# Branch C's query projections one by one, lower bounds in layer 0's MLP, and three changes of tiles in a hybrid encoder

## The chip, the cores and the metric

The kernel runs on one core of a Trainium2 chip as one program. Its engines are TensorE (PE, with weight loads shown as PEld), VectorE (DVE), ScalarE (ACT), GpSimd (POOL) and SyncE (SP); each takes its instructions in the order in which they stand in its queue. The metric is the device time of one execution in microseconds (us), and the profile is of one execution of its own.

## What is computed

A bidirectional encoder of two layers on 512 positions of 1024 channels. The reference, cut to what bears on the change:

```
for l in range(DEPTH):
    xn = rms_norm(x, ln1[l])
    z = xn @ w_in[l]                 # all branches' inputs at once
    a_q, a_i, a_ff, a_fb, a_g, b_u, b_v, c_q, c_k, c_v, gz = jnp.split(z, offsets, axis=-1)
    o_a = hgrn2_bidirectional(a_q, a_i, a_ff, a_fb, lower[l])   # 4 heads, both directions
    ...
    qh = partial_rope(c_q.reshape(bsz, s_len, C_QHEADS, C_HDIM), pos)   # 8 heads of 64
    y_c = window_attention(qh, kh, vh, sink[l])                 # |i - j| <= 128
    merged = gates[..., 0] * (y_a @ w_br[l, 0]) + gates[..., 1] * (y_b @ w_br[l, 1]) + gates[..., 2] * (y_c @ w_br[l, 2])
    x = x + merged @ w_out[l]
    x = x + jnp.square(jax.nn.relu(rms_norm(x, ln2[l]) @ w_up[l])) @ w_down[l]
p = softmax(lb_logits, axis=0); cum = cumsum(p, axis=0)
lower = cum - cum[0:1]               # 0 in layer 0: only layer 1 needs the lower bounds
```

## The kernel before

Each weight comes from memory as a chunk of 128x1024 (`wr` or `wq`, loads on SP's queue), is rounded by ACT (`wh`, L210) and its remainder is taken by DVE (`wl`, L211). A projection of 128 output channels is then 24 matmuls of 512 columns, three for each of eight parts of the inner dimension (L215 to L217), into one bank of PSUM; `evac` multiplies it by the norm's factor on DVE (L739) and frees the bank. The banks "m", from which most projections come, are two, so a projection waits for the evacuation of the last but one.

The order on each engine is not the order of the code. A scheduler places the instructions by priorities and a timeline of its own: what is written earlier has the higher priority, `hp()` raises it, and `with later(30000)` lowers it, so that the work in it (`fill`, the projections and gates of branch B) stands between other work. Where a tile's slots are taken (`SLOTS`, a number for each tag), a new tile of that tag waits for a release.

A layer runs in this way. First come the products common to all (`seven`), then head 0 of branch A (`a_head`) with branch B's mixing. `project(1)` follows, then the projections `ck`, `cv` and all four `cq` of branch C, each for two heads. From there `head(1)`, `head(2)`, `head(3)` go through `overlap`: seven levels of one head of A, each with attention matmuls `at` and sums over `ex` on DVE (L614), together with the tail of the head before (`kT`, `stp`, `av`, `oT`) and with one step of `c_run`, which is one pair of score blocks of C (`sc`, softmax on DVE and ACT, then `pT` and `po`). `c_q(j)` rotates a query: `rot` shuffles it on DVE, multiplies by `sin_t` on DVE and by `cos_t` on POOL (L950), adds on DVE, and splits it into halves on ACT and DVE (L988, L989). Between heads stand `fill(0, 1)`, `fill(2, 3)`, and at the end `fill(4, 5, 6, 7)`; each number is a projection `gz`, a product `yB` and a store to `mgd` on POOL's queue. Last come `gate_a` (`ag`), branch C's gated product (`yC`; gates are loaded to `th` from `thd` on POOL's queue, the first half is kept in `kept`, the second is stored to `mcd`), branch A's product (`yA`), the transposes `mT`, the output projection `wo` and the MLP (`up`, and `dA`, `dB`, `dC`).

`lower_bounds` makes three 128x8 constants from the logits in `vec_t`: small DVE rows, two Exp and two Ln on ACT, each change of function with a table load. It is written behind head 0 of layer 0, and its first tile is of the tag "a", which the pool of the branches owns.

Of the kernel before, what the change touches and what calls it, by code (L numbers as in the profile page):

```python
# [7 lines left out]
F32R = mybir.dt.float32r  # L8
# [52 lines left out]
def trunk(tc, xT, xt, ws, vec, fnb, bsb, snk, wst, rope, cmask, amask, ident, out):  # L61
# [4 lines left out]
    def pool(**kw):  # L66
# [13 lines left out]
    SLOTS = {"x": 16, "l": 8, "l2": 4, "tv": 8, "rb": 1, "jk": 1,  # L80
             "xs": 16, "zt": 6,
             "yh": 8,
             "q": 2, "a": 6, "ao": 1, "g": 2, "ch": 10,
             "yi": 16, "th": 8, "mg": 4,
             "h": 22}

# [6 lines left out]
    def nm(s):  # L93
        ctr[0] += 1
        return f"{s}_{ctr[0]}"

    def T(tag, name, dt=F32):
        where = part[HOME[tag]] if tag in HOME else sb
        return where.tile([P, S], dt, tag=tag, bufs=SLOTS[tag], name=nm(name))
# [22 lines left out]
    def SM(tag, w):  # L122
        return pad.tile([P, w], F32, tag="sm_" + tag, bufs=4 if tag == "lb" else NSM, name=nm(tag))
# [61 lines left out]
    def wload(*key):  # L185
        if key in ready:
            return ready.pop(key)
        with hp():
            raw = sb.tile([P, CW], F32, tag="wr", bufs=WR, name=nm("wr"))
            nc.sync.dma_start(raw, ws[CHUNK[key]])  # L190
            return wsplit(raw)
# [35 lines left out]
    def proj(xs, name, *key, bank="m"):  # L227

        return proj_w(xs, name, wload(*key), bank=bank)

    def proj_w(xs, name, w, koff=0, bank="m"):
        hi, lo = w
        pt = PT(bank, name)
        for k, x in enumerate(xs):
            c = slice((koff + k) * P, (koff + k + 1) * P)
            mm3(pt, hi[:, c], lo[:, c], x[0], x[1], k == 0, k == len(xs) - 1)
        return pt
# [251 lines left out]
    def lower_bounds():  # L489

        a, b = vec_t[:, 42:50], vec_t[:, 50:58]
        V = nc.vector
        m = T("a", "lbm")[:, 0:8]
        V.tensor_tensor(m, a, b, ALU.max)
        ea, eb = SM("lb", 8), SM("lb", 8)
        V.tensor_tensor(ea, a, m, ALU.subtract)
        V.tensor_tensor(eb, b, m, ALU.subtract)
        nc.scalar.activation(ea, ea, AF.Exp)
        nc.scalar.activation(eb, eb, AF.Exp)
        s = SM("lb", 8)  # L500
        V.tensor_tensor(s, ea, eb, ALU.add)
        V.reciprocal(s, s)
        V.tensor_tensor(ea, ea, s, ALU.mult)
        V.tensor_tensor(eb, eb, s, ALU.mult)
        lb = SM("lb", 8)
        V.tensor_tensor(lb, ea, eb, ALU.add)
        V.tensor_tensor(lb, lb, ea, ALU.subtract)
        om = SM("lb", 8)
        V.tensor_scalar(om, lb, -1.0, 1.0, ALU.mult, ALU.add)
        res = []  # L510
        for i, src in enumerate((om, lb)):
            g, z = SM("lb", 8), SM("lb", 8)
            V.tensor_scalar(z, src, 0.0, -1.0e30, ALU.is_le, ALU.mult)
            V.tensor_scalar(g, src, 1e-38, None, ALU.max)
            nc.scalar.activation(g, g, AF.Ln)
            r = cst.tile([P, 8], F32, name=f"lbr{i}")
            V.tensor_tensor(r, g, z, ALU.add)
            res.append(r)
        dl = cst.tile([P, 8], F32, name="lbd")
        V.tensor_tensor(dl, res[0], res[1], ALU.subtract)  # L520
        return res[0], res[1], dl
# [155 lines left out]
    def steps(run, n):  # L677
        for _ in range(n):
            with hp():
                next(run)  # L680

    def overlap(run, tail, side):

        for i in range(len(LEVELS)):
            steps(run, 1)
            if i < 4:
                steps(tail, 1)
            if i:
                next(side, None)


    begin("wq")
# [11 lines left out]
    raw, hi, lo = sb.tile([P, CW], F32, tag="wr", bufs=WR, name=nm("wr")), *whl()  # L704
# [21 lines left out]
    lbs = None  # L726
# [6 lines left out]
    for l in range(DEPTH):  # L733
        xs = n1.xs

        def evac(pt, tag, name):
            t = T(tag, name)
            with hp():
                nc.vector.tensor_tensor(t, pt, n1.rb, ALU.mult)  # L739
            return t  # L740
# [111 lines left out]
        for u in range(3):  # L852
            nxt = uload(l, "un", u + 1) if u < 2 else None
# [29 lines left out]
        oa = []  # L883
        run = a_head(l, 0, *head_0, vt, oa)
        steps(run, len(LEVELS))
        if l == 0:
            lbs = lower_bounds()

        for i in range(4):
            gelu2(bu[i])  # L890
        for t in range(4):
# [54 lines left out]
        def rot(z):  # L946
            sh = T("g", "sh")
            nc.vector.stream_shuffle(sh, z, list(range(8, 16)) + list(range(8)) + list(range(16, 32)))
            nc.vector.tensor_tensor(sh, sh, sin_t, ALU.mult)
            nc.gpsimd.tensor_tensor(z, z, cos_t, ALU.mult)  # L950
            nc.vector.tensor_tensor(z, z, sh, ALU.add)
            return z
# [2 lines left out]
        def project(h):  # L955
            return a_ffb(h), evac(proj(xs, "q", l, "q", h), "q", "q")

        def head(h, gq):
            nonlocal run
            nxt = a_head(l, h, *gq, vt, oa)  # L960
            overlap(nxt, run, banded)
            run = nxt

        head_1 = project(1)
        lo64, hi64 = slice(0, 64), slice(64, 128)
        ck = evac(proj(xs, "ck", l, "ck"), "ch", "ck")
        cvT = evac(proj(xs, "cv", l, "cv"), "ch", "cv")
        cq = [evac(proj(xs, "cq", l, "cq", j), "ch", "cq") for j in range(4)]
        ck = rot(ck)
        k2 = [T("tv", "k2", F32R), T("tv", "k2", F32R)]  # L970

# [10 lines left out]
        nc.scalar.copy(cv, pt)  # L982

        def c_q(j):
            z = rot(cq[j])
            qs = [T("ch", "q2", F32R), T("ch", "q2", F32R)]
            for h, (r, o) in enumerate(((lo64, hi64), (hi64, lo64))):
                nc.scalar.copy(qs[h][r], z[r])  # L988
                nc.vector.tensor_tensor(qs[h][o], z[r], qs[h][r].bitcast(F32), ALU.subtract)  # L989
            return qs  # L990
# [61 lines left out]
        def fill(*ds):  # L1052
            with later(30000):
                for d in ds:
                    merge_b(d)
# [13 lines left out]
            c_out(*prev)  # L1069

        banded = c_run()
        head(1, head_1)
        fill(0, 1)
        head(2, project(2))
        fill(2, 3)
        head(3, project(3))
# [4 lines left out]
        with later(30000):  # L1081
            for h in range(4):
                gate_a()

            ys = y_split(yc, "yh")
            kept = []
            for fl in range(2):
                th = gates("ch", 0, fl)
                pts = proj_tok(ys, "yC", (l, "y", 2, fl), 0)
                for t in range(4):  # L1090
                    if fl == 0:
                        kept.append(T("tv", "mC"))
                    m = th[t] if fl else kept[t]
                    with hp():
                        nc.vector.scalar_tensor_tensor(m, th[t], 1.0, pts[t], ALU.add, ALU.mult)
                    if fl:
                        nc.gpsimd.dma_start(mcd[:, t], m)
        ys = []
        for h in range(4):
            nc.vector.scalar_tensor_tensor(oa[h], oa[h], 0.5, sg[h], ALU.mult, ALU.mult)  # L1100
            hi, lo = T("tv", "yh", F32R), T("l", "yl", F32R)
            split(oa[h], hi, lo)
            ys.append((hi, lo))
        end("br")
# [53 lines left out]
        i = proj_part(n2.xs, *first[0], range(4))  # L1158
# [51 lines left out]

        for qd in range(4):
            hs, nh = [], [0]

            def new():
                nh[0] += 1
                return T("jk" if nh[0] == 1 else "rb" if nh[0] > 27 else "l2" if nh[0] > 23 else "h", "sh", F32R)

            for f in range(8):
                if qd == 0 and f < 3:
                    pt = first[f][0]  # L1220
                    proj_part(n2.xs, *first[f], range(4, KT))
                else:
                    pt = proj(n2.xs, f'up{qd}', l, "up", qd, f, bank="c" if qd == 0 and f == 3 else "m")
                if f == 0:
                    raw = uload(l, "dn", qd)
                u = Z()
                with hp():
                    nc.scalar.activation(u, pt, AF.Relu)
                    nc.scalar.activation(u, u, AF.Square)
                    if f % 2 == 0:  # L1230
                        hs.append(left_first(new, u))
                    else:
                        left_second(new, hs[-1], u)
                if f == (6 if qd == 0 else 4):
                    with tc.issue_after(hs[1]["i"].ins) if qd == 0 else contextlib.nullcontext():
                        early_sums(raw)
            if qd == 3:
                if last:
                    for fl in range(2):
                        fn_t.append(Z())  # L1240
                        nc.sync.dma_start(fn_t[fl], bass.AP(tensor=fnb.tensor, offset=fnb.offset + fl * S, ap=[[0, P], [1, S]]))
                else:
                    nxt = uload(l + 1, "un", 0)
            down(qd, raw, hs, acc, xr, r2, nr2, done, last)
# [129 lines left out]
```

## Time and profile before

| What | us or share |
|---|---|
| median of 3 runs (1717.69 to 1720.3) | 1719.31 |
| the profiled execution | 1723.92 |
| its span, first to last instruction | 1722.1 |
| mean granted TensorE clock | 0.993 |
| PE busy | 1686.2 (98%) |
| DVE busy | 1297.3 (75%) |
| ACT busy | 1017.0 (59%) |
| POOL busy | 137.3 (8%) |

Times in the views count from the first instruction. The branches of layer 0 run from about 186 to 430, those of layer 1 from about 1040 to 1300; the rest is the common products and the MLP. In a view by stretches PE's pauses are the stretch less its busy time, and PEclk is the share of full clock that was granted. A row of the timeline has its start, its duration, and in brackets the idle time of the engine just before it and what ended it.

### The profile page before, as it was taken

The page shows a single profiled execution, that of the slowest core. Times are in us where ns is not written, and L with a number is a line of the kernel's source. Part 1 is how long each engine was busy: PE and PEld are TensorE (multiplying, and loading weights), DVE is VectorE, ACT ScalarE, POOL GpSimd, SP SyncE. Part 2 cuts the span into 40 slices and gives each one's busy share as a digit, 9 for nine tenths or more (in the row PEclk, how much of TensorE's full clock was granted, in tenths as well). Part 3 has the DMA queues.
Part 4 walks back from the last instruction along what each step waited for, and adds up shares of the span by engine and source line. Part 5 has one row for each costly group of instructions (what it writes and reads, how often), then busy time and mean ns, then how long its engine had stood idle before and what let it go on. Part 6 is the DMA issues. An engine that isn't in the chain of part 4 may idle for free.

```text
span 1722.1 us, 21872 instructions
## 1 busy us (share of the span) xinstructions
PE 1686.2 (98%) x8024; PEld 1407.6 (82%) x8024; DVE 1297.3 (75%) x2009; ACT 1017.0 (59%) x1717; POOL 137.3 (8%) x199
## 2 busy tenths in 40 slices
PE   8999989999999999999999999999999999999998
PEld 7888878888778888888888788778887888888886
DVE  7996997775566758686889869968845667686867
ACT  7665677765235554545665757588753355545454
POOL 0011111100210000000010111110003100000001
PEclk9999999999999999999999999999999999999999
DMA  9342212222545323232323422122325452223321
GB/s 332 98 144 92 86 58 102 68 92 74 186 181 183 110 99 98 98 98 98 135 98 122 148 103 74 56 92 80 101 74 183 164 195 98 98 98 98 112 72 49
DMA packets 57003, 195.84 MB, mean 114 GB/s; under 512 B 7648, under 2 KB 8032, under 8 KB 56896
## 3 DMA queue, kind: packets, MB, share of 16 engines
q1 hardware_dynamic: 44640, 154.72, 26.7%
q0 software_dynamic: 11968, 39.20, 6.4%
q8 instruction: 63, 1.03, 0.2%
q10 hardware_dynamic: 288, 0.52, 0.1%
q14 instruction: 44, 0.36, 0.1%
HBM read 175.54 MB, written 18.87 MB: 113 GB/s over the span
## 4 chain that ended last, share of the span: by engine, by line
PE 79%; issue 7%; DVE 6%; ACT 4%; DMA 2%; POOL 1%; POOLq 0%; SPq 0%; ACTq 0%; DVEq 0%
PE up L216 7%; PE up L215 7%; PE up L217 7%; PE dA L430 3%; PE dA L431 3%; PE dA L432 3%; PE at L572 2%; PE wo L265 2%; PE wo L266 2%; PE wo L267 2%; PE dC L431 2%; PE dC L430 2%; PE dC L432 2%; PE po L1039 2%; PE f L215 1%
## 5 line engine op out<-in xcount | busy, mean ns | idle before, releaser
L210 ACT CAST wh<-wq 128x1024 fp32r<-128x1024 f32 x201 | 211.5, 1053 | 206.7 <-PE dA L431 48.3
L211 DVE TENSOR_TENSOR wl<-wq,wh 128x1024 fp32r<-128x1024 f32 x201 | 244.9, 1221 | 114.8 <-ACT wh L210 113.7
L211 DVE TENSOR_TENSOR wl<-wr,wh 128x1024 fp32r<-128x1024 f32 x166 | 204.2, 1231 | 136.1 <-ACT wh L210 135.8
L210 ACT CAST wh<-wr 128x1024 fp32r<-128x1024 f32 x166 | 174.1, 1050 | 223.7 <-PE up L216 69.8
L215 PE MATMUL up<-xh,wh 128*128 128x512 f32 x512 | 199.4, 389 | 0.0
L216 PE MATMUL up<-xl,wh 128*128 128x512 f32 x512 | 199.2, 389 | 0.0
L217 PE MATMUL up<-xh,wl 128*128 128x512 f32 x512 | 198.2, 389 | 0.0
L215 PEld LDWEIGHTS up<-xh,wh 128*128 128x128 f32 x512 | 96.1, 188 | 19.9
L217 PEld LDWEIGHTS up<-xh,wl 128*128 128x128 f32 x512 | 96.1, 188 | 19.9
L216 PEld LDWEIGHTS up<-xl,wh 128*128 128x128 f32 x512 | 96.1, 188 | 19.8
L430 PE MATMUL dA<-wh,sh 128*128 128x512 f32 x256 | 99.7, 390 | 0.0
L431 PE MATMUL dA<-wh,sh 128*128 128x512 f32 x256 | 99.6, 389 | 0.0
L432 PE MATMUL dA<-wl,sh 128*128 128x512 f32 x256 | 92.6, 389 | 0.0
L614 DVE TENSOR_TENSOR ex<-ex 128x512 f32<-128x512 f32 x112 | 77.9, 712 | 1.3 <-ACT key L594 0.9
L572 PE MATMUL at<-qt,kt 128*128 128x128 f32 x448 | 62.6, 276 | 2.7 <-DVE at L577 0.9
L572 PEld LDWEIGHTS at<-qt,kt 128*128 128x128 f32 x448 | 58.0, 191 | 6.2 <-DVE at L577 1.8
L285 POOL TENSOR_TENSOR rs<-ms,mhalf_t 128x4 f32<-128x4 f32 (+2 forms) x15 | 17.7, 1181 | 560.2 <-DVE ms L283 547.1
L586 ACT ACTIVATE qt<-ex 128x512 f32<-128x512 f32 x56 | 37.6, 672 | 39.3 <-DVE ex L614 28.8
L1008 DVE CUSTOM_DVE_ANT_0 sc<-sc,cmask,snk_t 128x256 f32<-128x256 f32 (+1 forms) x64 | 34.5, 545 | 30.6 <-PE pT L1034 28.1
L432 PEld LDWEIGHTS dA<-wl,sh 128*128 128x128 f32 x256 | 48.1, 188 | 10.0
L430 PEld LDWEIGHTS dA<-wh,sh 128*128 128x128 f32 x256 | 48.1, 188 | 10.0
L431 PEld LDWEIGHTS dA<-wh,sh 128*128 128x128 f32 x256 | 48.1, 188 | 9.9
(404 smaller groups left out, 4417.0 us busy)
## 6 DMA issues: line engine op xcount, KB each, us to landing
wr<-in_ws_dram SPq DMA_DIRECT2D x166, 512.0 KB, 3.3
wq<-in_ws_dram SPq DMA_DIRECT2D x117, 512.0 KB, 4.3
thd<-zt POOLq DMA_DIRECT2D x32, 256.0 KB, 2.5
th<-thd POOLq DMA_DIRECT2D x32, 256.0 KB, 4.1
mgd<-mg POOLq DMA_DIRECT2D x16, 256.0 KB, 2.4
mB<-mgd POOLq DMA_DIRECT2D x16, 256.0 KB, 5.3
x<-in_xT_dram SPq DMA_DIRECT2D x8, 256.0 KB, 6.1
xt<-in_xt_dram SPq DMA_DIRECT2D x8, 256.0 KB, 7.3
```

The source lines that it names most:

```text
L210: nc.scalar.copy(hi, raw)
L211: nc.vector.tensor_tensor(lo, raw, hi.bitcast(F32), ALU.subtract)
L215: nc.tensor.matmul(pt, whi, xhi, start=first, stop=False)
L216: nc.tensor.matmul(pt, whi, xlo, start=False, stop=False)
L217: return nc.tensor.matmul(pt, wlo, xhi, start=False, stop=last)
L430: nc.tensor.matmul(pt, xh[:, t], hi[:, c], start=start and k == 0, stop=False, skip_group_check=True)
L431: nc.tensor.matmul(pt, xl[:, t], hi[:, c], start=False, stop=False, skip_group_check=True)
L432: nc.tensor.matmul(pt, xh[:, t], lo[:, c], start=False, stop=k == 3, skip_group_check=True)
L572: nc.tensor.matmul(pt[:, c], kk(st), qq[:, c], start=True, stop=True)
L586: nc.scalar.activation(qt.rearrange(shp, b=nb, h=2), e_q, AF.Exp)
L614: nc.vector.tensor_tensor(o_ap, o_ap, ap_of(ex, i_, [[istep, 2]] + z), ALU.add)
L1008: nc.vector.tensor_tensor_reduce(s[:, :nk], pt[:, :nk], cmask_t[:, mo:mo + nk], 0.125, snk_t[:, l * 8 + hd:l * 8 + hd + 1], ALU.add, ALU.m ...
```

## The change

`c_q(j)` projects its own query now, so `cq` 0 is made at the first step of `c_run` and each other one at the second of the four score steps of the query before. `fill(0)` and `fill(1)` are called inside head 1's `overlap`, after its levels 2 and 5, and no longer behind it. `lower_bounds` is written in the MLP of layer 0, and its first tile comes from the pool `SM`, so that nothing but `vec_t` holds it. Branch C's tag "ch" has 7 tiles and not 10; `kept` takes tiles of "l" and the remainders `yl` of branch A's products tiles of "tv".

```
-             "q": 2, "a": 6, "ao": 1, "g": 2, "ch": 10,
+             "q": 2, "a": 6, "ao": 1, "g": 2, "ch": 7,
...
-        m = T("a", "lbm")[:, 0:8]
+        m = SM("lbm", 8)
...
-    def overlap(run, tail, side):
+    def overlap(run, tail, side, between):
...
             if i:
                 next(side, None)
+            if i in between:
+                between[i]()
...
-        if l == 0:
-            lbs = lower_bounds()
...
-        def head(h, gq):
+        def head(h, gq, between={}):
...
-            overlap(nxt, run, banded)
+            overlap(nxt, run, banded, between)
...
-        cq = [evac(proj(xs, "cq", l, "cq", j), "ch", "cq") for j in range(4)]
...
         def c_q(j):
-            z = rot(cq[j])
+            z = rot(evac(proj(xs, "cq", l, "cq", j), "ch", "cq"))
...
-        head(1, head_1)
-        fill(0, 1)
+        head(1, head_1, {2: lambda: fill(0), 5: lambda: fill(1)})
...
-                        kept.append(T("tv", "mC"))
+                        kept.append(T("l", "mC"))
...
-            hi, lo = T("tv", "yh", F32R), T("l", "yl", F32R)
+            hi, lo = T("tv", "yh", F32R), T("tv", "yl", F32R)
...
         for qd in range(4):
             hs, nh = [], [0]
+            if l == 0 and qd == 1:
+                lbs = lower_bounds()
```

On DVE in layer 1, the rows up to the evacuation `gz` for which PE's next projection waits (`q` with two numbers is a query's half, `sc`, `mx` and `es` belong to the softmax). Before:

```order
L989 TENSOR_TENSOR q_1926_9325<-cq_9119,q_1926_9325 64x512
L637 COPY st_9281<-stp_9277 128x128
L989 TENSOR_TENSOR q_1950_9413<-cq_9152,q_1950_9413 64x512
L989 TENSOR_TENSOR q_1951_9414<-cq_9152,q_1951_9414 64x512
L989 TENSOR_TENSOR q_2013_9640<-cq_9185,q_2013_9640 64x512
L577 COPY_PREDICATED at_9244<-amask_t,at_9293 128x512
L644 TENSOR_TENSOR qd_9316<-qd_9316,q_8157 128x384
L587 TENSOR_TENSOR qt_9434<-qt_9434,q_9020 128x512
L641 SCALAR_TENSOR_TENSOR st_9281<-st_9281,ms_9267,stp_9277 128x128
L614 TENSOR_TENSOR ex_8973<-ex_8973 128x2x32x8
L989 TENSOR_TENSOR q_2014_9641<-cq_9185,q_2014_9641 64x512
L739 TENSOR_TENSOR gz_9692<-gz_9667,rb_7749 128x512
```

Now, up to the second `gz`, for which the third `cq` projection waits:

```order
L614 TENSOR_TENSOR ex_8973<-ex_8973 128x2x64x4
L1011 TENSOR_TENSOR es_9233<-snk_t,mx_9231 128x2
L577 COPY_PREDICATED at_9112<-amask_t,at_9161 128x512
L614 TENSOR_TENSOR ex_8973<-ex_8973 128x2x64x4
L637 COPY st_9149<-stp_9145 128x128
L1006 ISA sc_9293,mx_9287<-sc_9290,cmask_8673,snk_t 128x384
L1006 ISA mx_9287 128x1
L1006 ISA sc_9298,mx_9287<-sc_9295,cmask_8673,snk_t 128x384
L1006 ISA mx_9287 128x1
L644 TENSOR_TENSOR qd_9184<-qd_9184,q_8157 128x384
L1013 TENSOR_TENSOR es_9233<-es_9233,su_9232 128x2
L741 TENSOR_TENSOR gz_9620<-gz_9595,rb_7749 128x512
```

Five remainders of the first three queries stood ahead of the first `gz`; now score rows of the first query stand ahead of the second `gz`, and the third and fourth query are not yet projected.

On POOL in layer 0, from the rotation of `ck` on (`key` and `rs` belong to the heads of A, `mgd` and `th` are the DMAs of branch B's and C's gates). Before:

```order
L950 TENSOR_TENSOR ck_1787<-ck_1787,cos_1384 128x512
L976 MEMSET kl_1961 64x512
L976 MEMSET kl_1962 64x512
L950 TENSOR_TENSOR cq_1853<-cq_1853,cos_1384 128x512
L950 TENSOR_TENSOR cq_1886<-cq_1886,cos_1384 128x512
L950 TENSOR_TENSOR cq_1919<-cq_1919,cos_1384 128x512
L934 DMA mgd<-mg_2448 128x512
L934 DMA mgd<-mg_2498 128x512
L950 TENSOR_TENSOR cq_1952<-cq_1952,cos_1384 128x512
L285 TENSOR_TENSOR rs_2118<-ms_2116,mhalf_t 128x4
L1048 DMA th_4015<-thd 128x512
L1048 DMA th_4017<-thd 128x512
```

Now:

```order
L949 TENSOR_TENSOR ck_1753<-ck_1753,cos_1384 128x512
L974 MEMSET kl_1795 64x512
L974 MEMSET kl_1796 64x512
L949 TENSOR_TENSOR cq_1918<-cq_1918,cos_1384 128x512
L949 TENSOR_TENSOR cq_2040<-cq_2040,cos_1384 128x512
L933 DMA mgd<-mg_2121 128x512
L933 DMA mgd<-mg_2336 128x512
L949 TENSOR_TENSOR cq_2406<-cq_2406,cos_1384 128x512
L285 TENSOR_TENSOR rs_1985<-ms_1983,mhalf_t 128x4
L596 TENSOR_TENSOR key_2553<-key_2553 128x512
L949 TENSOR_TENSOR cq_2852<-cq_2852,cos_1384 128x512
L933 DMA mgd<-mg_3041 128x512
```

The third query's multiply moved behind the first two stores to `mgd`, the fourth behind head 0's `rs` and head 2's `key`.

On PE at the end of layer 1's branches, around the last `po` and head 3's `av` (`pT` is the transpose ahead of `po`, `oT` that behind `av`). Before:

```order
L658 MATMUL av_10893<-st_10868,qd_10872 128x128
L658 MATMUL av_10893<-st_10886,qd_10890 128x128
L658 MATMUL av_10893<-vt_7833,at_10515 128x128
L658 MATMUL av_10893<-st_10868,qd_10872 128x128
L1034 MATMUL pT_10831<-id_t,sc_10782 128x128 x2
L1039 MATMUL po_10835<-pT_10826,cvt_9242 128x256 x2
L671 MATMUL oT_10916<-id_t,ao_10914 128x128 x4
L265 MATMUL yC_11303<-wh_11339,yh_11291 128x512
```

Now:

```order
L266 MATMUL yC_11304<-wh_11309,yl_11284 128x512
L267 MATMUL yC_11304<-wl_11310,yh_11283 128x512
L266 MATMUL yC_11306<-wh_11309,yl_11284 128x512
L1037 MATMUL po_10835<-pT_10826,cvt_9110 128x256 x2
L267 MATMUL yC_11306<-wl_11310,yh_11283 128x512
L658 MATMUL av_10893<-st_10886,qd_10890 128x128
L658 MATMUL av_10893<-vt_7618,at_10515 128x128
L658 MATMUL av_10893<-st_10868,qd_10872 128x128
L658 MATMUL av_10893<-st_10886,qd_10890 128x128
```

`po` stood right behind `pT` and `oT` right behind `po`; now 21 rows of `yC` stand between `pT` and `po`, and `av` follows `po`, with 24 rows of `yC` between `av` and `oT`.

In the start of the program the lower bounds' rows stand now on DVE and ACT beside the first input tiles, since nothing holds them there: on ACT two Exp rows ahead of the first `xh`, and a table load and two Ln rows ahead of the cast `wh` of the second weight.

## The prediction

> **What bounds the kernel now.** I read the page's busy shares first, then stretches by time, then PE's own waits in order of time, then DVE's rows ahead of the longest of them.
>
> ```profile
> PE 1686.2 (98%) x8024; PEld 1407.6 (82%) x8024; DVE 1297.3 (75%) x2009; ACT 1017.0 (59%) x1717; POOL 137.3 (8%) x199
> ```
> ```profile
> core 0: us, PE busy (x) PEld busy (x) DVE busy (x) ACT busy (x) POOL busy (x), PEclk, DMA share, GB/s
> 186.00:216.00 30.00, 29.31 (x149) 24.50 (x147) 28.94 (x43) 20.22 (x33) 6.57 (x5) 1.00 0.27 88
> 216.00:250.00 34.00, 29.40 (x143) 24.03 (x144) 32.48 (x71) 23.18 (x42) 3.65 (x3) 0.95 0.21 71
> 296.00:430.00 134.00, 133.50 (x751) 115.57 (x749) 94.21 (x216) 91.12 (x230) 11.01 (x15) 1.00 0.24 80
> 560.00:600.00 40.00, 40.00 (x178) 33.15 (x177) 27.92 (x36) 23.26 (x33) 0.00 (x0) 1.00 0.31 105
> 1040.00:1076.00 36.00, 36.00 (x185) 30.61 (x185) 35.78 (x54) 28.92 (x43) 5.54 (x5) 1.00 0.25 83
> 1076.00:1100.00 24.00, 20.43 (x97) 16.58 (x96) 23.72 (x42) 12.92 (x22) 3.82 (x2) 0.86 0.22 72
> 1100.00:1162.00 62.00, 60.17 (x320) 50.79 (x319) 45.31 (x101) 47.83 (x105) 7.72 (x9) 1.00 0.23 78
> 1279.00:1300.00 21.00, 19.00 (x98) 15.69 (x97) 10.23 (x20) 8.85 (x25) 1.04 (x1) 0.92 0.15 51
> ```
> PE is the bound: in the MLP (560 to 600) it never stops, at 40/178 = 0.225 us for a 512-column matmul. The change removes no PE work, so it can give back only PE's pauses. They stand where the branches overlap: idle 0.69 + 4.60 us at 186 to 250, 3.57 at 1076 to 1100, 1.83 at 1100 to 1162, 2.00 at 1279 to 1300. In the first stretches DVE is full (32.48 of 34, 35.78 of 36, 23.72 of 24 us), while later in the same branch it has room (94.21 of 134). PE's waits there:
>
> ```profile
> 208.50 1.13 PE L572 MATMUL at<-qt,kt 128*128 128x128 f32 x8 [0.47 <-DVE qt L587]
> 240.10 0.94 PE L634 MATMUL stp<-vt,kd 128*128 128x128 f32 x6 [1.49 <-ACT kd L631]
> 243.18 0.52 PE L215 MATMUL gz<-xh,wh 128*128 128x512 f32 x1 [2.15 <-DVE gz L739]
> ...
> 438.45 1.20 PE L265 MATMUL yC<-wh,yh 128*128 128x512 f32 x4 [1.27 <-ACT yh L273]
> ...
> 1093.02 0.55 PE L629 MATMUL kT<-id_t,kd 128*128 128x128 f32 x3 [2.09 <-DVE at L577]
> 1096.36 0.80 PE L215 MATMUL gz<-xh,wh 128*128 128x512 f32 x1 [0.58 <-DVE gz L739]
> ...
> 1293.10 1.13 PE L1039 MATMUL po<-pT,cvt 128*128 128x256 f32 x4 [1.27 <-ACT pT L1035]
> 1294.96 1.11 PE L671 MATMUL oT<-id_t,ao 128*128 128x128 f32 x4 [0.73 <-DVE ao L667]
> ```
> The long ones are one thing in both layers: the second gate projection of branch B waits for the evacuation of the first, which stands last in a full DVE queue. After each long pause the clock is halved for a while:
>
> ```profile
> 243.53:246.94 3.41, 3.41 (x10) 2.63 (x9) 3.41 (x12) 2.50 (x4) 0.04 (x1) 0.50 0.49 153
> 438.00:442.00 4.00, 3.55 (x16) 2.94 (x17) 2.54 (x5) 1.12 (x2) 0.00 (x0) 1.00 0.24 95
> 1093.45:1100.27 6.82, 5.67 (x17) 4.51 (x16) 6.76 (x17) 2.24 (x5) 0.07 (x1) 0.50 0.24 77
> 1294.83:1298.25 3.42, 3.29 (x9) 2.53 (x10) 3.21 (x6) 2.51 (x5) 0.00 (x0) 0.50 0.02 5
> ```
> At half clock the busy part costs double: 3.41/2 = 1.7, 5.67/2 = 2.8 and 3.29/2 = 1.65 us are lost. The 1.27 us pause before 438.45 was followed by none.
>
> **The change part by part.** Its main part spreads DVE's work. DVE's rows, start to start:
>
> ```profile
> 217.43 0.68 DVE L739 TENSOR_TENSOR cq<-cq,rb 128x512 f32<-128x512 f32 x1
> 218.03 0.54 DVE L644 TENSOR_TENSOR qd<-qd,q 128x384 f32<-128x384 f32 x1
> 218.50 0.68 DVE L951 TENSOR_TENSOR cq<-cq,sh 128x512 f32<-128x512 f32 x1
> 219.10 1.21 DVE L211 TENSOR_TENSOR wl<-wr,wh 128x1024 fp32r<-128x1024 f32 x1
> 220.24 0.68 DVE L614 TENSOR_TENSOR ex<-ex 128x512 f32<-128x512 f32 x1
> 220.84 0.15 DVE L501 TENSOR_TENSOR lb<-lb,lb 128x8 f32<-128x8 f32 x1
> 220.93 0.00 DVE L948 LOAD_MASK_SELECT sh<-cq  x1
> 220.93 0.73 DVE L948 STREAM_SHUFFLE sh<-cq 128x512 f32<-128x512 f32 x1
> 221.55 0.18 DVE L502 RECIPROCAL lb<-lb 128x8 f32<-128x8 f32 x1
> 221.69 0.69 DVE L949 TENSOR_TENSOR sh<-sh,sin 128x512 f32<-128x512 f32 x1
> 222.30 1.78 DVE L587 TENSOR_TENSOR qt<-qt,q 128x512 f32<-128x512 f32 x1
> 224.00 0.15 DVE L503 TENSOR_TENSOR lb<-lb,lb 128x8 f32<-128x8 f32 x1
> ...
> 235.10 2.12 DVE L989 TENSOR_TENSOR q<-cq,q 64x512 fp32r<-64x512 f32 x3
> ```
> ```profile
> 221.74 1.79 POOL L950 TENSOR_TENSOR cq<-cq,cos 128x512 f32<-128x512 f32 x1 [7.34 <-DVE lb L502]
> ```
> A 512-column row takes 0.60 us, a weight remainder 1.14, a shuffle 0.62, a query half's remainder 2.12/3 = 0.71, a lower-bound row 0.09. While POOL multiplied (221.74 to 223.53) the row at 222.30 took 1.70 instead of 0.60: each such multiply costs DVE 1.10.
>
> *Layer 0's full stretch.* I count DVE's rows from the evacuation of head 1's q to the evacuation that ends the long wait: before, the first gz; after, the second gz, for which the third cq projection waits. Out of that count go one weight remainder (1.14), two cq evacuations (1.20), a shuffle, a sine product and an add (1.82), two query remainders (1.42), 14 lower-bound rows (1.26): 6.8. Into it come a gz evacuation, a merge and an ex row (1.80), four score rows, two 256 and two 384 wide (I take 0.53 each, estimated from 0.60 for 512: 2.1), three tiny ones (0.27): 4.2. So DVE needs 2.6 less, and 1.10 less again, since two of the queries' POOL multiplies fall in it and not three. PE reaches the place sooner: 48 cq matmuls (10.8) and three state products (0.7) leave, 36 of gz and yB (8.1) and eight more score matmuls (1.6, at most at 0.2 each) come, 1.8 less. Wait: -2.6 - 1.1 + 1.8 = **-1.9**, of 5.29.
>
> *Layer 1's full stretch.* The same without the lower bounds (out 5.5), and a qt, an ex and a state row (0.60 + 0.60 + 0.3, the last estimated from the 0.54 above) fall behind the place, so out 7.0; in 3.6, without the ex row. -7.0 + 3.6 - 1.1 + 1.8 = **-2.7**, of 3.57.
>
> *Clock.* In layer 1 what is left (0.9) is a short pause, so I take the 2.8 as gone; in layer 0 3.4 us stay, in smaller pieces, and I take half of 1.7: **-3.65** (bounds 0 and -4.5). The Trainium skill, "TensorE: Matmul & The Clock Gate", Part 1, says instead that the clock falls after an idle window of about 3.4 us whose phase runs free, so that the same kernel differs from run to run. Here 2.15 us idle was enough; by its free phase the clock term may be absent from the runs compared, which is a rival below.
>
> *Layer 1's end.* At 1293 the last pT stands right ahead of its po, and av right ahead of oT, so PE waits for ACT and DVE twice. Now 21 yC matmuls (4.7 us) stand between pT and po and 24 (5.4 us) between av and oT, and ACT's copy and the way from av to oT run beside them. Both waits and the clock behind them go: -2.00 - 1.65 = **-3.65** (bounds 0 and -3.65).
>
> *Lower bounds.* They depend on one constant alone and stand at the very start now, with one of their two table loads; before:
>
> ```profile
> L515 ACT ACT_TABLE_LOAD x2: 1283/1283/1283, 234.0 to 244.7; - x2
> ```
> ```profile
> 10.76 1.03 ACT L210 CAST wh<-wr 128x1024 fp32r<-128x1024 f32 x1
> ...
> 14.18 0.39 PE L215 MATMUL bu<-xh,wh 128*128 128x512 f32 x1
> ```
> At the start the load and two Ln rows (1.28 + 2 x 0.2 = 1.7) push the second weight's cast, done at 11.79 and first read at 14.18: 2.4 us of cover, cost **0** (bounds 0 and +1.7, without the cover). The Trainium skill, "ScalarE: Activation LUTs", What ACT_TABLE_LOAD costs, adds a drain of about 1.38 us to each load; then 3.1 stand against 2.4 and the start costs +0.7. In this trace a load takes 1.28 and what the drain adds is not seen apart.
>
> From ACT's rows between 234 and 247 four loads go, two for Ln and two back to exp. The 1.49 us wait for kd at 240.10 goes with them; DVE's wait behind it begins sooner by as much, so nothing is added to the count.
>
> *Tiles.* kept in "l", yl in "tv" and seven "ch" tiles: the last two of the four second-half gate loads now wait for po and for the first half's multiply. The second half's 48 yC matmuls (10.8 us) hide them. Behind them on POOL stand the mcd stores, and in layer 1 head 3's rs, which needs av, itself behind the same po on PE:
>
> ```profile
> DMA to landing us min/median/max: 2.9/4.1/7.0
> ```
> Cost **0** (bounds 0 and 0; if the cover went, 4.1 per layer). The second half of the xr loads waits for the mT transposes instead of yA; a whole wo half (96 matmuls, 21.6 us) lies ahead of their use: 0.
>
> *New waits of the new order.* Not shown anywhere; the nearest row is the 1.83 us idle at 1100 to 1162, which one layer's later heads cost. Bounds 0 and 2 x 1.83 = 3.7; I take **+1.5**, since DVE keeps more work there.
>
> Sum: -1.9 - 2.7 - 3.65 - 3.65 + 0 + 1.5 = -10.4 us. The profiled execution took 1723.92 (span 1722.1), 4.6 above the median 1719.31, so 1713.5 in a profile and **1708.9** as the median. 0.2% (3.4 us) is about what a measurement here can tell from no change.
>
> **The rivals.** *Clock stays.* The half-rate stretches come all the same, wherever their phase puts them: without 3.65 and the end's 1.65 the sum is -5.1, 1714.2. For it: 3.4 us of pauses remain in layer 0. Against: all three followed about 2 us of idle in one pause or in two close ones (1.27 + 0.73), and the single 1.27 before 438.45 had none. The skill's page named above speaks for it.
>
> *The wait only moves.* The branch's DVE rows are the same in number; what leaves the full stretch comes back at heads 2 and 3. If it meets PE there, as at 1100 to 1162, both full stretches' gains (1.9 + 2.7 + 3.65) come back as waits and only the end's 3.65 is left, with 1.5 to pay: 1717.2. Against it: DVE is 70% busy there.
>
> *Slower: the scores wait for their query.* PE takes its rows in order, and a score now stands behind projection, evacuation, shuffle, sine, POOL's multiply, add, casts and remainders: 0.68 + 0.73 + 0.68 + 1.79 + 0.68 + 2 x 0.71, and two casts (estimated at half of the 1.03 of a 1024-column one): 7.0 us. In the new order PE's rows between a cq projection and its first score sum to 17.8 us for the first and 46 to 74 for the others (0.225 a 512-column row), before 30 to 137. It decides once DVE's backlog and POOL's queue take the chain past 17.8; a POOL row alone was held 7.34 us by DVE above. Each whole chain exposed costs 7.0, eight in all; two cancel the sum with 3.6 to spare (1722.9), four give 1736.9. I price it at two to four.
>
> **How the numbers follow.** Forecast 0.56 (1703 to 1714), clock stays 0.16 (1712 to 1716), wait moves 0.16 (1715 to 1722), slower 0.12. Faster by over 0.2% (below 1715.9): 0.56 + 0.16 and 0.02 of the third, 0.74; same 0.14; slower 0.12. The range leaves out the slow tail and a little below: 1703 to 1719.5.
>
> **What would show it.** Right: after, the second gz's and third cq's waits under 3.5 us in layer 0 and under 1 in layer 1, clock 1.00 where layer 1 had 0.86, no pause at po and oT of layer 1, no lower-bound row at 210 to 250. Wrong: PE idle of over 2 us at new places between 250 and 430 or 1100 and 1280, waits of sc on DVE's q remainders, or PE pausing before 20 us.

## The result, and the profile after

The changed kernel takes 1726.38 us in the median (1723.8 to 1727.71, 6 runs), the kernel before 1719.88 (1717.69 to 1721.78, 6 runs): a ratio of 1.0034, 95% interval 1.0024 to 1.0045. It is slower by 6.5 us, where 1708.9 was forecast. Its profiled execution took 1727.65 (span 1725.8, mean granted clock 0.998).

The engines' busy times of the page after:

```profile
PE 1697.0 (98%) x8024; PEld 1403.3 (81%) x8024; DVE 1296.9 (75%) x2009; ACT 1013.5 (59%) x1715; POOL 135.7 (8%) x199
```

PE's pauses shrank as the prediction wanted, from 1722.1 - 1686.2 = 35.9 us to 1725.8 - 1697.0 = 28.8. PE's busy time grew by 10.8, although the number of its records is the same and its clock is better. So the loss is no wait of PE. The same stretches as in the prediction, after:

```profile
186.00:216.00 30.00, 29.66 (x152) 24.60 (x151) 28.95 (x43) 21.30 (x28) 5.00 (x4) 1.00 0.21 71
216.00:250.00 34.00, 31.99 (x169) 26.14 (x168) 33.73 (x65) 22.06 (x48) 4.35 (x4) 1.00 0.27 93
1076.00:1100.00 24.00, 22.27 (x114) 18.48 (x113) 23.77 (x49) 14.91 (x30) 2.60 (x3) 1.00 0.23 79
1100.00:1162.00 62.00, 60.50 (x337) 51.76 (x336) 50.41 (x110) 49.84 (x108) 7.16 (x7) 1.00 0.22 72
1279.00:1300.00 21.00, 20.05 (x103) 16.68 (x102) 13.43 (x22) 9.92 (x23) 2.19 (x3) 1.00 0.22 76
```

In every one of them PE is busier than before, and the clock is 1.00 where it was 0.95, 0.86 and 0.92. PE's waits of the timeline after, in order of time:

```profile
242.58 0.50 PE L215 MATMUL cq<-xh,wh 128*128 128x512 f32 x1 [0.58 <-DVE gz L741]
...
474.89 1.25 PE L1112 MATMUL mT<-id_t,mC 128*128 128x128 f32 x8 [1.27 <-DVE mB L1117]
...
1078.77 0.50 PE L215 MATMUL yB<-yh,wh 128*128 128x512 f32 x1 [1.20 <-DVE cq L741]
1094.82 0.50 PE L215 MATMUL cq<-xh,wh 128*128 128x512 f32 x1 [0.53 <-DVE gz L741]
...
1146.03 1.13 PE L1037 MATMUL po<-pT,cvt 128*128 128x256 f32 x4 [1.25 <-ACT pT L1033]
...
1296.39 0.50 PE L265 MATMUL yC<-wh,yh 128*128 128x512 f32 x1 [0.95 <-DVE mC L1092]
1333.94 1.71 PE L1112 MATMUL mT<-id_t,mC 128*128 128x128 f32 x8 [3.26 <-DVE mB L1117]
```

None of the new ones reaches 1.3 us; those of `mT`, 1.27 and 3.26, are old ones, 2.61 and 2.47 before. What went wrong shows where nothing waits and nothing was changed, in the MLP of layer 0. Before, and then after:

```profile
560.00:840.00 280.00, 280.00 (x1239) 231.91 (x1238) 205.90 (x269) 148.16 (x203) 1.15 (x2) 1.00 0.31 103
```
```profile
560.00:840.00 280.00, 280.00 (x1222) 229.06 (x1221) 204.31 (x264) 146.87 (x201) 1.15 (x2) 1.00 0.31 100
```

PE is busy for all 280 us of both, at full clock, and gets through 1222 matmuls in place of 1239. The groups by line, kept apart by shape, tell which are slower (the last numbers: busy us, mean ns of one). Before:

```profile
L215 PE MATMUL up<-xh,wh 128*128 128x512 f32 x512 | 199.4, 389 | 0.0
L430 PE MATMUL dA<-wh,sh 128*128 128x512 f32 x256 | 99.7, 390 | 0.0
L430 PE MATMUL gA<-wh,xs 128*128 128x512 f32 x96 | 37.5, 390 | 0.9 <-ACT wh L210 0.9
L430 PE MATMUL gA<-wh,xh 128*128 128x512 f32 x32 | 12.9, 404 | 0.4
```

After:

```profile
L215 PE MATMUL up<-xh,wh 128*128 128x512 f32 x512 | 199.4, 389 | 0.0
L430 PE MATMUL dA<-wh,sh 128*128 128x512 f32 x256 | 101.3, 396 | 0.0
...
L430 PE MATMUL gA<-wh,xs 128*128 128x512 f32 x96 | 38.1, 397 | 0.9 <-ACT wh L210 0.9
...
L430 PE MATMUL gA<-wh,xh 128*128 128x512 f32 x32 | 12.9, 403 | 0.3
```

A matmul has a stationary operand, the 128x128 block that PEld loads, named last in a row, and a moving one, here of 512 columns. The same line, L430, is slower with a stationary `sh` or `xs` and not with `xh`. Tiles are cut from pools, stretches of on-chip memory, and a pool starts where the ones ahead of it end. `xh`, `wh` and `wl` lie in the pool `sb`; `sh` and `xs` lie in the pools behind the small pool `pad`. The change's `m = SM("lbm", 8)` opens a new tag in `pad`: three buffers of 32 bytes, 96 bytes of each partition. The pools behind it, with all tiles of the branches and the MLP, began at byte 126464 and begin at 126560 now.

### The profile page after: what moved, and what is told of

The parts are those of the page before. It is cut to its first block, busy times and chain, and to the rows that moved or that the text cites. A ratio compares the mean times of both kernels' runs of the same rounds, so it can differ in the third digit from the quotient of the medians.

```text
span 1725.8 us, 21884 instructions
## 1 busy us (share of the span) xinstructions
PE 1697.0 (98%) x8024; PEld 1403.3 (81%) x8024; DVE 1296.9 (75%) x2009; ACT 1013.5 (59%) x1715; POOL 135.7 (8%) x199
## 4 chain that ended last, share of the span: by engine, by line
PE 69%; issue 11%; DVE 8%; ACT 6%; DMA 3%; POOL 2%; POOLq 0%; SPq 0%; DVEq 0%; ACTq 0%
PE up L217 7%; PE up L216 7%; PE up L215 7%; PE dA L430 3%; PE dA L432 3%; PE dA L431 3%; PE at L572 2%; PE dC L431 2%; PE dC L430 2%; PE dC L432 2%; DVE ex L614 2%; PE wo L267 2%; PE wo L265 2%; PE wo L266 2%; PE po L1037 1%
## 5 line engine op out<-in xcount | busy, mean ns | idle before, releaser
L211 DVE TENSOR_TENSOR wl<-wq,wh 128x1024 fp32r<-128x1024 f32 x201 | 245.4, 1222 | 118.0 <-ACT wh L210 116.4
L430 PE MATMUL dA<-wh,sh 128*128 128x512 f32 x256 | 101.3, 396 | 0.0
L430 PEld LDWEIGHTS dA<-wh,sh 128*128 128x128 f32 x256 | 48.2, 188 | 11.3
L273 ACT CAST sh<-sf 128x512 fp32r<-128x512 f32 x64 | 39.6, 619 | 21.0 <-DVE sf L395 16.5
```

The source lines that it names most:

```text
L211: nc.vector.tensor_tensor(lo, raw, hi.bitcast(F32), ALU.subtract)
L273: nc.scalar.copy(hi, src)
L430: nc.tensor.matmul(pt, xh[:, t], hi[:, c], start=start and k == 0, stop=False, skip_group_check=True)
```

## The experiments

In each, "start to start" is the time between the starts of neighbouring matmuls, taken from the trace.

**1. The same instructions at other places.** Four kernels differ from the changed one, or from the one before, in bytes alone: every engine's rows are the same, in the same order.

```
a128: changed kernel;  bufs=4 if tag in ("lb", "lbm") else NSM          # +128 against before
b96, b64, b32: before;  pad.tile([P, 24], ...), ([P, 16], ...), ([P, 8], ...)   # unused
```

> The changed kernel, instruction for instruction; only the small pool takes 128 bytes more per partition than in the kernel before, where the change made it 96 more, so that every tile behind it starts at a multiple of 128 again. Addresses theory (the 512-column matmuls that read a tile at a start of 32 modulo 64 run at about 233 ns instead of 227, some 2690 of them by 6.1 ns, 16.5 us): 1726.4 - 16.5 = 1709.9, the groups dA, dB, dC, gA<-xs, wo, yB, yC back at 227. Rival, the new order of the work itself costs the 6.5 us (waits and queues): 1726, the groups stay at 233.

> The kernel before, instruction for instruction, with 96 unused bytes per partition added in the small pool, so that its branch and MLP tiles lie where the change puts them. Addresses theory: 1719.9 + 16.5 = 1736.4, and dA, dB, dC, gA<-xs, wo, yB, yC at 233. Rival, the new order costs it: 1719.9, all groups at 227.

> The kernel before with 64 unused bytes added. If the price hangs on the start modulo 64: 1719.9 and 227 ns. If any start off a multiple of 128 (or 512) pays: about 1736 and 233 ns, or something between. Rival, order alone: 1719.9.

> The kernel before with 32 unused bytes added. If the price hangs on the start modulo 64, the same as with 96: about 1736 and 233 ns. If it hangs on 128 in steps, another price than with 96. Rival, order alone: 1719.9.

Measured, each beside new runs of the kernel before (in this set 1720.03): b96 1736.65 (ratio to it 1.0096, 1.0082 to 1.011), b64 1735.56 (1.0087, 1.0074 to 1.01), b32 1734.66 (1.0084, 1.0071 to 1.0097), a128 1721.96 (1.0015, 1.0006 to 1.0025). The kernel before, with 96 unused bytes, shows the slower rows:

```profile
L215 PE MATMUL up<-xh,wh 128*128 128x512 f32 x512 | 199.3, 389 | 0.0
L430 PE MATMUL dA<-wh,sh 128*128 128x512 f32 x256 | 101.4, 396 | 0.0
```

So 96 bytes that nothing reads cost 16.6 us, as expected to 0.3 us, and at equal places the change is faster: 1726.38 against 1736.65. But modulo 64, and modulo 128, were wrong: 64 bytes cost as much, and with 128 the `dA` row still took 394 ns.

**2. 256 and 512 bytes, everything moved alike, and the lower bounds undone.**

```
a512, a256: changed kernel;  bufs=4 if tag == "lb" else 16 (8) if tag == "lbm" else NSM
c96: before;  cst.tile([P, 24], F32, name="gap_t")     # in the first pool: all tiles move by 96
a_lbback: changed kernel;  m = T("a", "lbm")[:, 0:8], lower_bounds() behind head 0 as before
```

> The changed kernel, instruction for instruction, with the small pool 512 bytes longer than before's, so that the tiles behind it start at the same places modulo 512 as in the kernel before. If the price goes by the start modulo 512 (128 bytes off still had 232 ns): all groups at 227, and 1726.4 - 16.5 = 1709.9, which is what the order of the work alone is worth. Rival: what was left with 128 bytes (1722) is the order's own cost: 1722 again, though the groups read 227.

> The changed kernel with the lower bounds as before: in layer 0's head 0, their maximum in one of the branch's big tiles; nothing in the small pool, so the tiles lie where they lay before. Addresses theory: groups at 227, 1709.9 and up to 3 more for the 14 lower-bound rows and the table loads in layer 0's full stretch (1.3 on DVE, 1.5 at kd). Rival (the order costs it): 1722 to 1726.

> The changed kernel, instruction for instruction, with the small pool 256 bytes longer than before's. If starts at multiples of 256 are free: groups at 227, about 1710. If only multiples of 512 are (a 128 x 128 block of 4-byte values takes 512 bytes of a partition): 231 to 234 ns, 1722 to 1726.

> The kernel before, instruction for instruction, with 96 unused bytes at the end of the first pool of all, so that every tile of the kernel is moved by 96 and none against another. If what counts is the start itself: all the 512-column matmuls of the kernel pay, the up projections too, some 6 500 by 6 ns: about 1719.9 + 39 = 1759. If what counts is how the two operands of a matmul lie to one another: all at 227, 1719.9.

Measured: a512 1711.17 (0.9945, 0.9931 to 0.9958), a256 1708.96 (one run), c96 1720.3 (one run), a_lbback 1716.0 (0.9979, 0.9967 to 0.9991), which fits neither of its two expectations. The `dA` rows with 512 bytes, and with everything moved by 96:

```profile
L430 PE MATMUL dA<-wh,sh 128*128 128x512 f32 x256 | 99.7, 389 | 0.0
```
```profile
L430 PE MATMUL dA<-wh,sh 128*128 128x512 f32 x256 | 99.7, 390 | 0.0
```

Three things follow. Multiples of 256 cost nothing. The start itself does not count, since c96 moves every tile to a start of 96 modulo 256 and pays nothing; what counts is how a matmul's operands lie to one another. And the changed kernel with its instructions untouched gains 9.5 us on the kernel before, once its tiles stand right. It beats both kernels, as pcq below does. Start to start, the groups that read a moved tile took in the changed kernel, against a512, 6.2 ns more in `dA`, `dB`, `dC` (1343 matmuls, 8.3 us), 6.9 with a stationary `xs` (576, 4.0), 5.9 in `wo` (384, 2.3), 6.0 in `yC` (192, 1.2) and 3.8 in `yB` (192, 0.7), where the moved tile is the moving operand: 16.4 us together. In the other 512-column groups the mean difference is 0.3 ns.

**3. The parts one by one,** all at before's places.

```
pcq: before, with the change's overlap(..., between), c_q(j) that projects, and the calls of fill
ptile: before;  kept.append(T("l", "mC")),  yl from T("tv", ...)
plb: before;  lower_bounds() in layer 0's MLP,  m = SM("gsc", 12)[:, 0:8]    # a tile that is there
```

> The kernel before with one part of the change alone: C's four query projections one by one ahead of their scores (with the first two groups of gates placed as in the change). Tiles and lower bounds as before, every tile starts where it did before. My prediction's steps give this part: layer 0's stretch about -0.6 (without the lower bounds' 1.3), layer 1's -2.7, clock -3.65, layer 1's end -3.65, new waits +1.5, together about -9: 1711. Rival, what the runs so far say by difference (the change without its lower bounds stood at 1716.0): 1715 to 1716, the rest of the gain being the lower bounds'.

> The kernel before with the tiles alone: the first half's gated products in the tiles of the other pool, the low parts of the yh split with the high ones, C's head outputs still in ten tiles. My prediction: 0, 1719.9 to 1720.7. Rival (the loads that now wait for other tiles come late and the transposes behind them wait): 1722 or more, with the wait at mT over 2.6 us.

> The kernel before with the lower bounds alone moved into layer 0's MLP code, their maximum in a tile that is already there, so nothing moves in memory. My prediction: -1.3 on DVE in layer 0's full stretch, -1.5 at kd, 0 to +1.7 at the start: 1717 to 1718. Rival, by difference of the runs so far: -4.8, 1715.

Measured: pcq 1709.56 (0.9938, 0.9926 to 0.9951), ptile 1721.31 (1.0006, 0.9996 to 1.0016), plb 1721.59 (1.001, 1.0 to 1.0019). The query projections, together with the new places of `fill(0)` and `fill(1)`, bring all the gain there is, 10.4 us; these two were not run apart. The lower bounds and the tiles bring nothing, alone perhaps a loss of one to two microseconds that these runs do not separate from none; for the lower bounds a gain of 2 to 3 was expected. That a_lbback stood 4.8 above a512 is therefore not the lower bounds' worth; see 5.

**4. The price by itself.** This kernel does nothing but rows of 96 matmuls.

```
for d in (32, 64, ..., 1024):  matmul(pt, sta[:, d//4 : d//4+128], mov[:, 0:512])   # x96
```

> Leaves all of the reference's work out: rows of 96 matmuls 128*128 by 128x512 in the kernel's number type, back to back with nothing beside them, the stationary block d bytes past the start of its tile (sta..x), or the moving one (mov..x), or both, or the two by turns (own..x: each matmul's two operands shifted alike, the next one's stationary not; cross..x: the other way round). Theory, the two operands' reads collide in SBUF by how they lie to one another modulo 256: 227 ns at 0, 256, 512, 768, 1024 and at both96x, 231 to 234 at 32, 64, 96, 128, 160, 192, 224, 288, 384 and for the moving one shifted. If what collides is the next weight load with the matmul that is running: own..x slow, cross..x at 227; if it is a matmul's own two operands, the other way round. Rival, the collision is with the other engines' or the DMAs' accesses to SBUF: 227 everywhere here.

Its groups, some of them (a prefix tells which operand is moved, the number by how many bytes; "nar" has 128 columns, "half" 256):

```profile
L80 PE MATMUL sta96x<-mov_t,sta_t 128*128 128x512 f32 x96 | 22.6, 397 | 0.0
L80 PE MATMUL own96x<-mov_t,sta_t 128*128 128x512 f32 x96 | 22.6, 396 | 0.0
L80 PE MATMUL mov32x<-mov_t,sta_t 128*128 128x512 f32 x96 | 22.6, 395 | 0.0
...
L80 PE MATMUL sta128x<-mov_t,sta_t 128*128 128x512 f32 x96 | 22.5, 395 | 0.0
...
L80 PE MATMUL cross96x<-mov_t,sta_t 128*128 128x512 f32 x96 | 22.2, 392 | 0.0
L80 PE MATMUL sta192x<-mov_t,sta_t 128*128 128x512 f32 x96 | 22.1, 392 | 0.0
...
L80 PE MATMUL both96x<-mov_t,sta_t 128*128 128x512 f32 x96 | 21.9, 389 | 0.0
L80 PE MATMUL even<-mov_t,sta_t 128*128 128x512 f32 x96 | 21.9, 389 | 0.0
L80 PE MATMUL sta256x<-mov_t,sta_t 128*128 128x512 f32 x96 | 21.9, 389 | 0.0
...
L80 PE MATMUL half0x<-mov_t,sta_t 128*128 128x256 f32 x96 | 11.7, 284 | 0.0
L80 PE MATMUL half96x<-mov_t,sta_t 128*128 128x256 f32 x96 | 11.4, 280 | 0.0
L80 PE MATMUL nar96x<-mov_t,sta_t 128*128 128x128 f32 x96 | 10.9, 275 | 0.0
L80 PE MATMUL nar0x<-mov_t,sta_t 128*128 128x128 f32 x96 | 10.8, 274 | 0.0
```

Start to start, without a row's first gaps, the mean is 226.7 ns at 0, 256, 768 and 1024, 227.0 at 512, and 226.8 with both moved by 96. It is 232.3 to 234.2 at 32, 64, 96, 128, 160, 224, 288 and 384 and with the moving operand moved, 228.9 at 192. With 256 or 128 columns nothing is lost. Besides PE only one copy of a single column on DVE follows each row of 96, so the rival, a collision with other engines or with DMAs, falls. Which two reads collide stays open: with each matmul's operands alike and the neighbour's not (own96x) it is 233.9, which speaks for the next weight load against the running matmul, but the other way round (cross96x) it is 230.0 and not 227, by turns 224 and 236. With 128 bytes the two are 228.4 (own128x) and 230.0 (cross128x), which speaks for neither.

**5. The tiles beside the new order.**

```
pcq_ch: pcq with "ch": 7
pcq_kept: pcq with kept.append(T("l", "mC")),  yl from T("tv", ...)
```

> The kernel before with the query projections one by one and seven of C's tiles in place of ten; the other tiles and the lower bounds as before; every tile behind starts at the same place modulo 256 as before. With ten it stood at 1709.6. My prediction: the two of four second-half gate loads that wait longer are hidden, 1709.6. Rival: they put the tail's transfers off, the weight load beside them lands late and the transposes mT of layer 0 wait some 5 us in place of 1.6, as in the change without its lower bounds: 1714 to 1716.

> The kernel before with the query projections one by one and the first half's gated products and the low parts in the other pool's tiles, C's tiles still ten, lower bounds as before. My prediction: 1709.6. Rival (these tiles, which put the input loads off until the transposes have read, cost what the change without its lower bounds shows): 1714 to 1716.

Measured: pcq_ch 1709.83 (0.9947, 0.9934 to 0.996), pcq_kept 1714.95 (0.9978, 0.9966 to 0.999). The seven tiles cost nothing, though in the profile of pcq_ch the first transposes wait 2.31 us; `kept` and `yl` cost 5.4 us on top of pcq, 5.1 against pcq_ch, which ran beside it. It lies in layer 0's tail: pcq_kept's first `yC` starts 1.0 us after pcq's, its last `wo` 7.8 after. In order of time, POOL's gate loads, DVE's product that waits for the first of them, the next weight's load, that weight's remainder on DVE, which stands ahead of `mB` in its queue, and PE's transposes, in pcq:

```profile
454.29 2.13 POOL L1049 DMA_DIRECT2D th<-thd  x4 [3.91 <-DMA mcd<-th]
```
```profile
457.51 0.69 DVE L1134 SCALAR_TENSOR_TENSOR th<-th,yA 128x512 f32<-128x512 f32 x1 [6.53 <-DMA th<-thd]
```
```profile
460.69 0.33 SPq L190 DMA_DIRECT2D wr<-in_ws_dram  x1
```
```profile
469.75 1.23 DVE L211 TENSOR_TENSOR wl<-wr,wh 128x1024 fp32r<-128x1024 f32 x1 [4.95 <-ACT wh L210]
```
```profile
471.62 1.25 PE L1115 MATMUL mT<-id_t,mC 128*128 128x128 f32 x8 [1.47 <-DVE mB L1120]
```

The same in pcq_kept:

```profile
459.20 2.13 POOL L1049 DMA_DIRECT2D th<-thd  x4 [4.87 <-PE yA L266]
```
```profile
462.42 0.69 DVE L1134 SCALAR_TENSOR_TENSOR th<-th,yA 128x512 f32<-128x512 f32 x1 [7.79 <-issue]
```
```profile
465.59 0.33 SPq L190 DMA_DIRECT2D wr<-in_ws_dram  x1
```
```profile
475.17 1.23 DVE L211 TENSOR_TENSOR wl<-wr,wh 128x1024 fp32r<-128x1024 f32 x1 [5.46 <-ACT wh L210]
```
```profile
477.04 1.33 PE L1115 MATMUL mT<-id_t,mC 128*128 128x128 f32 x5 [5.16 <-DVE mB L1120]
```

POOL's loads begin 4.9 us later, in both runs 0.70 behind the landing of the last store to `mcd` (453.59 and 458.50). That store needs the last `yC` matmul, ahead of which 16 rows of `yA` stand on PE in pcq_kept and 6 in pcq; it starts at 452.38 and not at 448.43 (1.0 of this is there at the first `yC`). DVE's product waits for the load, and a weight's remainder behind it in DVE's queue (ends at 460.66 and 465.57) frees one of the two buffers `wr`, for which the next weight's load waits. That weight lands 5.4 later (468.56 and 473.99): 4.9 of it is the later issue and only 0.5 a longer transfer (7.88 and 8.40). Its own remainder comes 5.4 later, `mB` is queued behind it, and PE waits 3.7 us longer; the clock was then halved for 6.8 us. a_lbback shows the same wait (4.89). In the changed kernel, where the lower bounds are moved too, the wait is 1.27 and in a512 none, so the tiles' cost hangs on the order that the scheduler finds around them: pcq 1709.56, all parts at right places 1711.17. These are single profiles; after and a512 have the same rows in the same order and differ in this wait. Why the moved lower bounds shift that order was not tried.

## Why the prediction was wrong, step by step

Its signs came out as right but for one: the third `cq` waits 0.58 and 0.53 us, the clock is 1.00, nothing pauses at layer 1's last `po` and its `oT`, no new wait reaches 2 us; only an earlier `po` of layer 1 waits, 1.25 us at 1146. The time was wrong all the same, because the failing step was the first of the argument: "The change removes no PE work, so it can give back only PE's pauses". It took PE's time per matmul as fixed, and of the line `m = SM("lbm", 8)` priced only the rows. The term that it lacks is 96 bytes, +16.4 us. Against before's profile, by terms:

- Layer 0's full stretch: predicted -1.9; idle at 186 to 250 went from 5.29 to 0.34 + 2.01 = 2.35, -2.9. The third `cq` waits where the second `gz` did.
- Layer 1's: predicted -2.7; idle at 1076 to 1100 went from 3.57 to 1.73, -1.8. Part of it is a new wait, 1.20, of `yB` for the evacuation of `cq`, which now comes late in DVE's queue.
- Clock: predicted -3.65; both half-rate stretches are gone, -4.5. Here "clock stays" did not happen: all seven profiles in the old order (before, c96, b96, b64, b32, ptile, plb) have a stretch at half clock that begins at 240 to 245 and one at 1091 to 1105, and none of the eight in the new order has one there.
- Layer 1's end: predicted -3.65. The waits at `po` and `oT` are gone, but `yC` waits 0.95 for DVE, and the transposes behind wait 3.26 and not 2.47: -1.05, -1.65 for the clock, +0.8, so -1.9. The clock's part is not the order's doing: c96, b96, b64 and b32 have the rows of before and the same pauses there (1.27 or 1.28, then 0.73), and no half-rate stretch follows. So the length of the pauses, by which the prediction argued against "clock stays", did not decide it.
- New waits: predicted +1.5; idle at 1100 to 1162 went from 1.83 to 1.50, -0.3. "The wait only moves" and "the scores wait for their query" did not happen: no `sc` waits. That the measured time lies among the prices of the second (1722.9 to 1736.9) is chance.
- Lower bounds at the start: predicted 0. The Ln rows and their table load stand right ahead of the second weight's cast, as argued. ACT's rows after, and the first matmul that reads the cast:

```profile
8.46 1.28 ACT L515 ACT_TABLE_LOAD   x1
9.75 0.21 ACT L515 ACTIVATE lb<-lb 128x8 f32<-128x8 f32 x1
...
12.42 1.03 ACT L210 CAST wh<-wr 128x1024 fp32r<-128x1024 f32 x1
```
```profile
13.51 0.50 PE L215 MATMUL bu<-xh,wh 128*128 128x512 f32 x1
```

  The Ln row starts 0.01 us behind the load, so the drain of 1.38 us that the Trainium skill, "ScalarE: Activation LUTs", What ACT_TABLE_LOAD costs, adds to each load is not seen here. PE lost under 0.3 us in this profile, and 1.24 in a512's.
- Tiles: predicted 0 within bounds of 0. As time, ptile alone is not told from 0, but beside the new order they cost 5.4 without the moved lower bounds. The prediction took the order around them as given and asked only whether each load has cover. With these tiles the scheduler put ten more rows of `yA` ahead of the last `yC`, and the stores to `mcd`, the gate loads, a weight's buffer and `mB` hang on it one behind the other. The `xr` loads, which it looked at, are not in that chain.

The terms but the tiles sum to -11.4; the first transposes' wait in layer 0 (2.61 before, 1.27 after) adds -1.3, and the operands' places +16.4: +3.7, which is the difference of the spans. That it agrees so closely is luck. Left out are the half-clock stretch at 479.05 to 482.46 and the `yC` wait of 1.27 before, both gone after, and on the other side a new wait of 1.10 at 178.87 and the 0.3 ns of the other matmuls. And the profiled execution of before was a long one, 4.0 us above its median, that of after 1.3, so the medians differ by 6.5: the 1.65 above, the stretch at 479 (1.7) and part of the 2.61 (1.16 to 1.54 in c96, b96, b64 and b32) belong to that execution.

Without the bytes the forecast would have stood as a sum: -10.4 there, and -9.5 measured for the whole change with 512 bytes. But single terms missed by 0.8 to 1.8, some one way and some the other, so that this agreement is partly luck too.

## What to carry to other kernels

When a change adds or drops a tile, compare where all tiles lie before and after, down to the byte: a 32-byte scratch tile in an early pool can slow thousands of matmuls that the diff never touches. If PE's busy time moves while its work does not, group its matmuls by the tiles they read; which operand the slower ones share points to the pool. Here 160 bytes more, up to a multiple of 256, took the loss away.

## What the runs showed of the hardware

A matmul of 128x128 by 512 columns in the fp32r type ran, in rows of equal ones, at one per 226.7 to 227.0 ns where its stationary and moving operands start at a distance that is a multiple of 256 bytes, and at one per 228.9 to 234.2 at the other multiples of 32 that were tried; with 256 columns (119.9 even, 117.3 at 96 bytes) and 128 (111.7 both) no such loss shows. The weight load's own record stays at 188 ns in both cases, so only the matmuls' rows show it. The Trainium skill, "TensorE: Matmul & The Clock Gate", Step-by-step: what each phase is for, says that loading the next tile's weights does not steal SBUF read bandwidth from the running matmul; at distances off 256 the runs differ from that, by some 6 ns of 227, if it is these two reads that collide, which the turns above leave open.
